# A SwiGLU step's two input products by seven block products of a 2x2 splitting

## The chip, the cores and the metric

One core of one Trainium2 chip, with TensorE (matmul), VectorE (DVE), ScalarE (ACT), GpSimd (POOL) and SyncE (SP, which issues most DMAs). The metric is device time in microseconds, measured in three runs: median 1006.16 us, from 1006.01 to 1006.53.

## The reference, cut to what matters

A decoder layer for 512 tokens of width 1024. It has two macaron half steps; each is a SwiGLU with 2816 hidden features. The second one is

```
h = h + 0.5 * swiglu(rmsnorm(h, g_ffn2), w1_b, w3_b, w2_b)
def swiglu(x, w1, w3, w2):
    return (jax.nn.silu(x @ w1) * (x @ w3)) @ w2
```

Before it stand the first half step and a mixer (attention beside a state-space model); after it a gated embedding and a last norm. Everything is float32. `w1` makes the gate product, `w3` the linear product; together they are 2 x 1024 x 2816 weights.

## The kernel before

Activations lie with features on the 128 partitions and the 512 tokens along the row. A float32 product is made of three TensorE products in a rounded format: each operand is split into a high part (rounded) and a low part (what is left), and `mm3` (lines 234 to 237) adds hi x hi, lo x hi and hi x lo in PSUM. So one block of 128x128 weights costs three matmuls, each with its own weight load. The normalized input is `n3.hl[k]`, k from 0 to 7, with high and low part side by side; the norm's factor per token, `nrm.r`, is multiplied in after the product.

The 2816 hidden features are 22 tiles of 128, in three parts of 7, 7 and 8 (`PARTS`). For each tile there is a unit for the gate product and one for the linear product, each of two steps (4 of the 8 k each, 12 matmuls of 512 columns a step). After a part's tiles come eight products with the second matrix `w2`, which add to the residual tiles `X[m]`. `ffn_units` (line 345) builds the units.

The order of all engines' work is written out by `run` (line 204): for each step it issues first the roundings of the next unit's weights (`split_w`, line 151: a ScalarE cast to the high part), then the evictions that are due (`evicts`), the generators in `chains`, the deferred work in `posts`, then the remainders of the weights (a VectorE subtraction to the low part, which is followed by the next weight DMA on SP), and then the step's matmuls. Each engine takes its instructions in this order and waits for semaphores where data are not there yet. Raw weights go through five buffers of 128x512 (`wraw`), rounded ones through four pairs (`whi`, `wlo`). After a tile's gate product, VectorE multiplies by `nrm.r` (`gate_a`), ScalarE takes tanh, VectorE forms the gate (`gate_b`), and after the linear product follow `lin_a`, `lin_b` and `lin_c`, with a ScalarE cast of the hidden tile between. GpSimd has no work in the second half step, apart from a norm's power.

The gate weights of the gated embedding (`u_g`) are rounded ahead, in units 20 to 15 from the end of the second half step (`U2[j // 2 - 20].extra`). At its end `last` (line 1372 on) makes one tile's product in two halves of 256 columns, with the same three terms.

Of the kernel before, what the change touches and what calls it, by code (L numbers as in the profile page):

```python
# [21 lines left out]
EPS = 1e-6  # L22
FIRST = [(0, 2), (2, 4), (4, 8)]
PREP = 5
FEW = 3
SCORES = [(n, n + 1, n + 2) for n in (0, 4, 8, 12)]
VALUES = [7, 11, 15, 18]
# [14 lines left out]
def hybrid_trunk_kernel(ctx: ExitStack, tc: tile.TileContext, xT, pT, w13a, w2a, w13b, w2b, wqk, wv, ws, wf,  # L42
# [71 lines left out]
    selr = const.tile([128, 8], F32R, name="selr")  # L114


    qsel = [const.tile([128, L], F32R, name=f"qsel{j}") for j in range(2)]
    kcum = [const.tile([128, L], F32R, name=f"kcum{j}") for j in range(2)]
    HALF = [slice(0, 64), slice(64, 128)]


# [1 line left out]
    class Unit:  # L123
        def __init__(self, srcs, steps, posts=(), need=None, alloc=None, ahead=True):
# [3 lines left out]
            self.parts = [None] * len(srcs)  # L128
            self.starts, self.extra = [], []

        def w(self, c, n=1):
            hi, lo = self.parts[c // 4]
            sl = slice((c % 4) * 128, (c % 4 + n) * 128)
            return hi[:, sl], lo[:, sl]

    RAWS = 5
    wseq, raws = [], {}
    dma_at = [0]

    def wdma():  # L140
        j = dma_at[0]
        if j >= len(wseq):
            return
        dma_at[0] += 1
        u, i = wseq[j]
        n = u.srcs[i].shape[-1]
        w = pool.tile([128, 512], F32, name=nm("wraw"), tag="wraw", bufs=RAWS)
        nc.sync.dma_start(w[:, 0:n], u.srcs[i])
        raws[(id(u), i)] = w

    def split_w(u, i):
        w = raws.pop((id(u), i))
        n = u.srcs[i].shape[-1]
        if u.alloc is not None:
            hi, lo = u.alloc()
        else:
            hi = pool.tile([128, 512], F32R, name=nm("whi"), tag="whi", bufs=4)
            lo = pool.tile([128, 512], F32R, name=nm("wlo"), tag="wlo", bufs=4)
        S.copy(hi[:, 0:n], w[:, 0:n])  # L159
        u.parts[i] = (hi, lo)  # L160

        def rest():
            tt(lo[:, 0:n], w[:, 0:n], raw32(hi[:, 0:n]), SUB)
            wdma()
        return rest

    evicts, posts, chains, low, late = [], [], [], [], []
# [19 lines left out]
    def convert(u, nxt, h):  # L187

        last = h == len(u.steps) - 1
        res = []  # L190
        if nxt is not None:
            res = [(nxt, i) for i in range(len(nxt.srcs)) if nxt.parts[i] is None and (i == h or last)]
        return res + [(v, i) for hh, v, i in u.extra if hh == h]

    def order_weights(units):
        seen = set()
        for u, nxt in zip(units, units[1:] + [None]):
            for h in range(len(u.steps)):
                for v, i in convert(u, nxt, h):
                    if (id(v), i) not in seen:  # L200
                        seen.add((id(v), i))
                        wseq.append((v, i))

    def run(units):
        while dma_at[0] < RAWS:
            wdma()
        for ui, u in enumerate(units):
            nxt = units[ui + 1] if ui + 1 < len(units) else None
            for f in u.starts:
                f()  # L210
            for h, step in enumerate(u.steps):
                rest = [split_w(v, i) for v, i in convert(u, nxt, h)] if u.ahead else []
                run_posts(evicts)
                advance(chains)
                while late:
                    late.pop(0)()
                run_posts(posts)
                for f in rest:
                    f()
                step(u)  # L220
                if not u.ahead:
                    for v, i in convert(u, nxt, h):
                        split_w(v, i)()
                if slot_no[0] % 4 != 3:
                    advance(low)
                advance(chains)
                if slot_no[0] % 4 != 3:
                    advance(low)
                slot_no[0] += 1
                for st_, d, f in u.posts:  # L230
                    if st_ == h:
                        evicts.append((slot_no[0] + d, f, u.need))
# [109 lines left out]

    PARTS = [range(0, 7), range(7, 14), range(14, 22)]

    def ffn_units(nrm, w13, w2, final, skip_first=False):
        units = []
        ready = lambda: nrm.r is not None
        for pi, part in enumerate(PARTS):
            hid = {}
            for f in part:  # L350
                box = {}

                def gate_a(box=box):
                    box["t"] = tmp(base="t1")
                    tt(box["t"], box[0], nrm.r, MUL)
                    box["h"] = tmp(base="th")
                    act(box["h"], box["t"], AF.Tanh, scale=0.5)

                def gate_b(box=box):
                    stt(box["t"], box["h"], 1.0, box["t"], ADD, MUL)  # L360

                def lin_a(box=box):
                    box["u"] = tmp(base="t3")
# [24 lines left out]
                for wi in range(2):  # L388
                    srcs = [w13[f, wi][:, c * 512:(c + 1) * 512] for c in range(2)]
                    units.append(Unit(srcs, gemm_steps(box, wi, nrm.pair, KD), [(1, d, fn) for d, fn in after[wi]], ready))  # L390
            f0, n = part[0], len(part)
            pair = lambda k, hid=hid, f0=f0: (hid[f0 + k][:, 0, :], hid[f0 + k][:, 1, :])
            done = pi == len(PARTS) - 1

            def res(box, m, done=done):
                def f():
                    stt(X[m], box[0], 0.5, X[m], MUL, ADD)
                    if done:
                        final(m)
                return f  # L400

            boxes = [{}, {}]

            def side(m, k0, k1, boxes=boxes, pair=pair, n=n):
                def f(u):
                    if k0 == 0:
                        boxes[m][0] = bank()
                    for k in range(k0, k1):
                        mm3(boxes[m][0], *u.w(m * 4 + k - k0), *pair(k), k == 0, k == n - 1)
                return f  # L410
            for k0, k1 in ((0, 4), (4, n)):
# [1013 lines left out]
    u_proj, p_load, p_prep = proj_units(pp)  # L1425
    u_os = out_units(wout[1], n_s, None)
    u_oa = out_units(wout[0], n_a, lambda m: n3.add(m, X[m]))
    U2 = ffn_units(n3, w13b, w2b, lambda m: n4.add(m, X[m]))
    u_g, g_load, g_last = gate_units(n4, pp)

    def chain_at(u, gen):
# [10 lines left out]
    u_qk[3][0].starts.append(p_load)  # L1442
    u_glu[1].starts.append(p_prep)
    chain_at(U2[0], n3.chain(wait=2))
    chain_at(u_g[0], n4.chain(wait=4, halved=True))
    u_g[0].starts.append(g_load)
    for j in range(12):
        U2[j // 2 - 20].extra.append((j % 2, u_g[j // 2], j % 2))


    fw = [[g4([128, KD, 128], dt, "fw") for dt in (F32, F32R, F32R)] for _ in range(2)]
# [156 lines left out]
```

## Time and profile before

| | |
|---|---|
| median of three runs | 1006.16 us |
| profiled execution | 1005.92 us |
| its span, first to last instruction | 1004.1 us |
| TensorE busy | 992.8 us, 99% |
| VectorE busy | 642.2 us, 64% |
| ScalarE busy | 418.8 us, 42% |
| GpSimd busy | 85.5 us, 9% |

The span and the device time differ by 1.8 us that lie around the instructions. Busy time of TensorE is modelled: matmuls are pipelined, so the time from one start to the next tells its pace, and the duration of one (0.39 us) is longer than that. A releaser behind an arrow is what ended the idle time before an instruction.

### The profile page before, as it was taken

The page shows a single profiled execution, that of the slowest core. Times are in us where ns is not written, and L with a number is a line of the kernel's source. Part 1 is how long each engine was busy: PE and PEld are TensorE (multiplying, and loading weights), DVE is VectorE, ACT ScalarE, POOL GpSimd, SP SyncE. Part 2 cuts the span into 40 slices and gives each one's busy share as a digit, 9 for nine tenths or more (in the row PEclk, how much of TensorE's full clock was granted, in tenths as well). Part 3 has the DMA queues.
Part 4 walks back from the last instruction along what each step waited for, and adds up shares of the span by engine and source line. Part 5 has one row for each costly group of instructions (what it writes and reads, how often), then busy time and mean ns, then how long its engine had stood idle before and what let it go on. Part 6 is the DMA issues. An engine that isn't in the chain of part 4 may idle for free.

```text
span 1004.1 us, 13381 instructions
## 1 busy us (share of the span) xinstructions
PE 992.8 (99%) x4800; PEld 826.8 (82%) x4800; DVE 642.2 (64%) x1252; ACT 418.8 (42%) x793; POOL 85.5 (9%) x87
## 2 busy tenths in 40 slices
PE   9999999999999999999999999999999999999996
PEld 7888888888878889887888888888888888888876
DVE  6668788767755555889987865443454436646443
ACT  6333233332244444469995443322333224434232
POOL 0440000001000001004651010000000000000000
PEclk9999999999999999999999999999999999999998
DMA  6433332323245332212212232333323334533101
GB/s 211 149 93 84 110 103 94 87 82 107 95 109 129 94 95 74 64 64 74 80 59 74 86 114 95 103 92 100 101 89 97 93 105 148 168 103 95 43 36 49
DMA packets 56915, 96.57 MB, mean 96 GB/s; under 512 B 10176, under 2 KB 14912, under 8 KB 56848
## 3 DMA queue, kind: packets, MB, share of 16 engines
q1 hardware_dynamic: 56432, 94.62, 30.9%
q0 software_dynamic: 416, 1.08, 0.4%
q8 instruction: 38, 0.62, 0.3%
q14 instruction: 29, 0.24, 0.1%
HBM read 92.41 MB, written 2.10 MB: 94 GB/s over the span
## 4 chain that ended last, share of the span: by engine, by line
PE 93%; DVE 3%; ACT 2%; issue 1%; DMA 1%; POOL 0%; SPq 0%; POOLq 0%; ACTq 0%; DVEq 0%
PE ps L235 29%; PE ps L237 29%; PE ps L236 29%; PE ps L1487 1%; PE ps L1098 1%; PE ps L1144 1%; PE ps L1143 0%; PE ps L315 0%; PE ps L329 0%; DVE lg L1074 0%; DVE qkhl L74 0%; PE ps L754 0%; DVE wlo L74 0%; PE ps L647 0%; DMA fw<-w13a 0%
## 5 line engine op out<-in xcount | busy, mean ns | idle before, releaser
L235 PE MATMUL ps<-xhl,whi 128*128 128x512 f32 x816 | 320.6, 393 | 0.0
L237 PE MATMUL ps<-xhl,whi 128*128 128x512 f32 x816 | 318.1, 390 | 0.0
L236 PE MATMUL ps<-xhl,wlo 128*128 128x512 f32 x816 | 317.9, 390 | 0.0
L159 ACT CAST whi<-wraw 128x512 fp32r<-128x512 f32 x324 | 195.8, 607 | 240.9 <-PE ps L237 177.7
L74 DVE TENSOR_TENSOR wlo<-wraw,whi 128x512 fp32r<-128x512 f32 x324 | 216.6, 673 | 5.8 <-ACT whi L159 5.6
L237 PEld LDWEIGHTS ps<-xhl,whi 128*128 128x128 f32 x816 | 153.2, 188 | 32.2
L235 PEld LDWEIGHTS ps<-xhl,whi 128*128 128x128 f32 x816 | 153.3, 188 | 32.0 <-issue 1.0
L236 PEld LDWEIGHTS ps<-xhl,wlo 128*128 128x128 f32 x816 | 153.4, 188 | 30.9
L235 PE MATMUL ps<-h,whi 128*128 128x512 f32 x352 | 137.4, 390 | 0.0
L237 PE MATMUL ps<-h,whi 128*128 128x512 f32 x352 | 137.1, 389 | 0.0
L236 PE MATMUL ps<-h,wlo 128*128 128x512 f32 x352 | 137.1, 389 | 0.0
L77 DVE SCALAR_TENSOR_TENSOR x<-ps,x 128x512 f32<-128x512 f32 x48 | 33.2, 691 | 95.2 <-PE ps L237 95.1
L77 DVE SCALAR_TENSOR_TENSOR t<-ps,rbc 128x512 f32<-128x512 f32 x44 | 30.3, 690 | 76.4 <-PE ps L237 76.4
L237 PEld LDWEIGHTS ps<-h,whi 128*128 128x128 f32 x352 | 66.1, 188 | 13.8
L235 PEld LDWEIGHTS ps<-h,whi 128*128 128x128 f32 x352 | 66.1, 188 | 13.7
L236 PEld LDWEIGHTS ps<-h,wlo 128*128 128x128 f32 x352 | 66.1, 188 | 13.6
L74 DVE TENSOR_TENSOR t<-ps,rbc 128x512 f32<-128x512 f32 x44 | 30.4, 690 | 71.2 <-PE ps L237 65.0
L80 ACT ACTIVATE th<-t 128x512 f32<-128x512 f32 x44 | 27.8, 633 | 91.1 <-DVE t L74 91.1
L369 ACT CAST h<-t 128x512 fp32r<-128x512 f32 x44 | 27.4, 622 | 80.6 <-DVE t L74 80.6
L319 POOL TENSOR_TENSOR rc<-ms,mhalf 128x4 f32<-128x4 f32 x6 | 8.1, 1345 | 519.3 <-DVE ms L318 519.3
L1090 POOL TENSOR_SCALAR lg<-lg,rs 128x128 f32<-128x128 f32 (+3 forms) x32 | 37.8, 1196 | 97.8 <-issue 78.6
L80 ACT ACTIVATE xhl<-x,colt 128x512 fp32r<-128x512 f32 x32 | 22.9, 725 | 48.2 <-DVE x L77 41.1
(254 smaller groups left out, 1105.0 us busy)
## 6 DMA issues: line engine op xcount, KB each, us to landing
wraw<-w13b SPq DMA_DIRECT2D x88, 256.0 KB, 2.9
wraw<-w13a SPq DMA_DIRECT2D x84, 256.0 KB, 2.8
wraw<-w2a SPq DMA_DIRECT2D x32, 256.0 KB, 2.7
wraw<-w2b SPq DMA_DIRECT2D x32, 256.0 KB, 2.7
wraw<-wqk SPq DMA_DIRECT2D x16, 256.0 KB, 2.8
wraw<-wout SPq DMA_DIRECT2D x16, 256.0 KB, 2.8
wraw<-wgate SPq DMA_DIRECT2D x16, 256.0 KB, 2.8
wraw<-w2a SPq DMA_DIRECT2D x16, 192.0 KB, 2.4
```

The source lines that it names most:

```text
L74: V.tensor_tensor(out, a, b, op)
L77: V.scalar_tensor_tensor(out, a, s, b, op0, op1)
L80: S.activation(out, in_, f, **kw)
L159: S.copy(hi[:, 0:n], w[:, 0:n])
L235: T.matmul(ps, lh, rh, start=start, stop=False)
L236: T.matmul(ps, ll, rh, start=False, stop=False)
L237: T.matmul(ps, lh, rl, start=False, stop=stop)
L369: S.copy(hl[:, 0, :], box["t"])
L1090: G.tensor_scalar(x, x, rs[h2][:, j:j + 1], None, MUL)
L1098: T.transpose(ps[:, j * 128:(j + 1) * 128], lg[h2][:, j * 128:(j + 1) * 128], ident)
L1144: T.matmul(po[:, j * 128:], vv, pl, start=False, stop=j == 3)
L1487: T.matmul(box0[wi], fw[wi][2 if i == 1 else 1][:, k], n1.pair(k)[i == 2], start=k + i == 0, stop=k + i == KD + 1)
```

## The change

`PLAIN = (4, 0, 0)`: in the second half step the first four tiles of the first part stay as they were; the other 3 + 7 + 8 = 18 tiles are made by `quick_units`. There the two products of a tile are taken as one product of 2x2 blocks: block rows are the gate and the (negated) linear features, the inner dimension is halved (k 0 to 3 and 4 to 7), block columns are the lower and the upper 256 tokens. With A11, A12 the gate weights for the two halves of k, A21, A22 the linear ones, xl, xu and yl, yu the input blocks, the seven products are

| i | weights | times |
|---|---|---|
| 0 | A11 | xl |
| 1 | S1 = A21 + A22 | xl - xu |
| 2 | S2 = S1 + A11 | xu - xl - yu |
| 3 | A12 | yl |
| 4 | S3 = A11 + A21 | yu - xu |
| 5 | S4 = A12 + S2 | yu |
| 6 | A22 | yu - xu + xl - yl |

Each takes 4 k of three matmuls with 256 columns. Products 0, 2, 4 and 6 accumulate in the left half of one PSUM bank, and ScalarE copies the half out after 0 (`p1`), 2 (`u2`) and 4 (`u3`); products 3 and 1, 5 lie in the halves of another bank, the right one copied after 1 (`p5`). VectorE puts the outputs together (`gate_a`, `lin_a`, `gate_c`, `lin_b`), now with one more multiplication by `nrm.r`.

The input sums are made once by `halves`, a chain in the first four tiles. S1, S3 and S4 are made by DMAs that GpSimd issues with `accum_op=ADD`, which read the second summand from HBM; S2 by an addition on GpSimd. When a weight is rounded is set by `SPLIT`, in steps from the tile's first product, and the first adding DMA by `FIRST_ADD`. Raw A11 blocks get two buffers of their own (`spare`); these four buffers hold `qsel` and `kcum` earlier on. Rounded weights use the `m2` buffers besides `whi` and `wlo`, so the gate weights of `u_g` are now rounded in units 8 to 3 from the end.

```diff
+PLAIN = (4, 0, 0)
@@
     def wdma():
+        while dma_at[0] < len(wseq):
+            u, i = wseq[dma_at[0]]
+            ring = "k" if isinstance(u, Quick) and i == 1 else "w"
+            done = rings[ring]
+            if len(done) >= SIZE[ring] and not done[len(done) - SIZE[ring]]:
+                return
...
@@
             for h, step in enumerate(u.steps):
...
+                rest += [f for f in [f() for f in u.hooks.get(h, [])] if f]
                 run_posts(posts)
@@
+    def halves(nrm, goff):
...
+        for k in range(4):
+            xa, xb, ta, tb = [tmp(base="xt") for _ in range(4)]
+            act(xa, X[k], AF.Copy, scale=colt[:, goff + k:goff + k + 1])
+            act(xb, X[k + 4], AF.Copy, scale=colt[:, goff + k + 4:goff + k + 5])
+            G.tensor_tensor(ta[:, 0:HT], xa[:, 0:HT], xa[:, HT:], SUB)
+            G.tensor_tensor(tb[:, 0:HT], xb[:, HT:], xa[:, HT:], SUB)
+            G.tensor_tensor(ta[:, HT:], xb[:, HT:], ta[:, 0:HT], ADD)
+            G.tensor_tensor(tb[:, HT:], ta[:, HT:], xb[:, 0:HT], SUB)
...
+            S.copy(a[:, 0, 0:HT], ta[:, 0:HT])
+            act(a[:, 0, HT:], ta[:, HT:], AF.Copy, scale=-1.0)
+            S.copy(b[:, 0, :], tb)
...
+    def quick_units(nrm, w13, fs, hid, before):
...
+        SPLIT = [-5, -4, -3, -2, 1, 2, 0]
+        FIRST_ADD = -10
...
+        def first_add(n):
+            q = tens[n]
+            return lambda: nc.gpsimd.dma_start(q.raw(A21), q.srcs[A22], accum_op=ADD) and None
...
+                S.copy(hi, src)
+                ops[n, i] = hi, lo
+                if i == 0:
+                    G.tensor_tensor(spare(n % 2), q.raw(A21), q.raw(A11), ADD)
+
+                def rest():
+                    tt(lo, src, raw32(hi), SUB)
+                    if i == 0:
+                        nc.gpsimd.dma_start(q.raw(A11), q.srcs[A21], accum_op=ADD)
+                    elif i == 2:
+                        nc.gpsimd.dma_start(spare(n % 2), q.srcs[A12], accum_op=ADD)
...
+                    for k in range(4):
+                        ks = slice(k * 128, k * 128 + 128)
+                        first = k == 0 and i < 2
+                        T.matmul(out, hi[:, ks], moving(i, k, 0), start=first, stop=False, skip_group_check=i > 1)
+                        T.matmul(out, lo[:, ks], moving(i, k, 0), start=False, stop=False, skip_group_check=i > 1)
+                        T.matmul(out, hi[:, ks], moving(i, k, 1), start=False, stop=k == 3, skip_group_check=i > 1)
...
+            def p1(box=box):
+                box["t"] = tmp(base="t1")
+                S.copy(box["t"][:, 0:HT], box[0][:, 0:HT])
...
+            def u2(box=box):
+                S.copy(box["t"][:, HT:], box[0][:, 0:HT])
...
+            def gate_a(box=box):
+                t = box["t"]
+                tt(t, box[1], t, ADD)
+                tt(t, t, nrm.r, MUL)
+
+            def lin_a(box=box):
+                u = box["u"]
+                tt(u[:, HT:], u[:, HT:], u[:, 0:HT], ADD)
+
+            def gate_b(box=box):
+                box["h"] = tmp(base="th")
+                act(box["h"], box["t"], AF.Tanh, scale=0.5)
+
+            def gate_c(box=box):
+                stt(box["t"], box["h"], 1.0, box["t"], ADD, MUL)
+                tt(box["t"], box["t"], nrm.r, MUL)
+
+            def lin_b(box=box):
+                h, t = box["h"], box["t"]
+                stt(h[:, HT:], box["u"][:, HT:], -0.5, t[:, HT:], MUL, MUL)
+                stt(h[:, 0:HT], box[0][:, 0:HT], -0.5, t[:, 0:HT], MUL, MUL)
...
+            d = (0, 0, 0, 1, 1) if last else (0, 1, 2, 3, 4)
+            u = Unit([], [product(i) for i in range(KINDS)],
+                     [(0, 0, p1), (1, 0, p5), (2, 0, u2), (4, 0, u3), (5, 0, gate_a), (5, 0, lin_a)]
+                     + [(6, e, fn) for e, fn in zip(d, (gate_b, gate_c, lin_b, hid_a, hid_b))])
@@
-    U2 = ffn_units(n3, w13b, w2b, lambda m: n4.add(m, X[m]))
+    U2 = ffn_units(n3, w13b, w2b, lambda m: n4.add(m, X[m]), plain=PLAIN)
@@
+    chain_at(U2[0], halves(n3, G_FFN2))
@@
-        U2[j // 2 - 20].extra.append((j % 2, u_g[j // 2], j % 2))
+        U2[j // 2 - 8].extra.append((j % 2, u_g[j // 2], j % 2))
```

## Rows read from the trace of the kernel before

**Rows 1.** The page's first two parts: busy time of each engine; granted clock in 40 slices.
```profile
PE 992.8 (99%) x4800; PEld 826.8 (82%) x4800; DVE 642.2 (64%) x1252; ACT 418.8 (42%) x793; POOL 85.5 (9%) x87
...
PEclk9999999999999999999999999999999999999998
```

**Rows 2.** The chain that ended last: share of the span by engine.
```profile
PE 93%; DVE 3%; ACT 2%; issue 1%; DMA 1%; POOL 0%; SPq 0%; POOLq 0%; ACTq 0%; DVEq 0%
```

**Rows 3.** One plain tile as a stretch: length, each engine's busy time, clock, DMA share, GB/s.
```profile
642.10:652.98 10.88, 10.88 (x49) 9.01 (x48) 5.78 (x9) 3.63 (x6) 0.00 (x0) 1.00 0.31 93
```

**Rows 4.** In order of time, plain tiles: start, duration (us), engine, line, operation, operands.
```profile
641.67 0.39 PE L237 MATMUL ps<-xhl,whi 128*128 128x512 f32 x1
...
642.10 0.69 DVE L77 SCALAR_TENSOR_TENSOR t<-ps,rbc 128x512 f32<-128x512 f32 x1 [2.75 <-PE ps L237]
...
652.98 0.69 DVE L77 SCALAR_TENSOR_TENSOR t<-ps,rbc 128x512 f32<-128x512 f32 x1 [2.76 <-PE ps L237]
```

**Rows 5.** In order of time, the 256-column matmuls and weight loads at the end.
```profile
990.83 0.28 PE L237 MATMUL ps<-gw,xhl 128*128 128x256 f32 x1
...
996.23 0.28 PE L237 MATMUL ps<-gw,xhl 128*128 128x256 f32 x1
...
990.84 0.19 PEld L235 LDWEIGHTS ps<-gw,xhl 128*128 128x128 f32 x1
```

**Rows 6.** In order of time, VectorE's followers, and gate product to tanh and back.
```profile
465.39 0.69 DVE L74 TENSOR_TENSOR wlo<-wraw,whi 128x512 fp32r<-128x512 f32 x1
465.99 0.68 DVE L77 SCALAR_TENSOR_TENSOR qk<-ps,rbc 128x512 f32<-128x512 f32 x1
...
480.60 0.40 DVE L74 TENSOR_TENSOR pb<-ps,pa 128x256 fp32r<-128x256 f32 x1
480.92 0.41 DVE L74 TENSOR_TENSOR pc<-ps,pc 128x256 fp32r<-128x256 f32 x1
...
960.81 0.69 DVE L77 SCALAR_TENSOR_TENSOR gt<-gt,pp 128x512 f32<-128x512 f32 x1 [1.59 <-ACT gt L80]
961.60 0.69 DVE L74 TENSOR_TENSOR o<-gt,ps 128x512 f32<-128x512 f32 x1
...
647.54 0.69 DVE L74 TENSOR_TENSOR t<-ps,rbc 128x512 f32<-128x512 f32 x1 [2.16 <-PE ps L237]
...
648.26 0.63 ACT L80 ACTIVATE th<-t 128x512 f32<-128x512 f32 x1 [2.78 <-DVE t L74]
...
648.93 0.70 DVE L77 SCALAR_TENSOR_TENSOR t<-th,t 128x512 f32<-128x512 f32 x1
```

**Rows 7.** In order of time, ScalarE operations that follow each other.
```profile
497.03 0.60 ACT L159 CAST whi<-wraw 128x512 fp32r<-128x512 f32 x1
497.54 0.36 ACT L1114 CAST pa<-ps 128x256 fp32r<-128x256 f32 x1
497.80 0.37 ACT L1114 CAST pc<-ps 128x256 fp32r<-128x256 f32 x1
```

**Rows 8.** GpSimd's one 512-wide addition (group by line), and VectorE beside GpSimd work.
```profile
L1380 POOL TENSOR_TENSOR o<-o,gfb 128x512 f32<-128x512 f32 x1 | 1.3, 1295 | 5.3 <-ACT gt L80 5.3
...
473.70 0.96 DVE L74 TENSOR_TENSOR wlo<-wraw,whi 128x512 fp32r<-128x512 f32 x1
...
491.35 1.08 DVE L74 TENSOR_TENSOR wlo<-wraw,whi 128x512 fp32r<-128x512 f32 x1
```

**Rows 9.** DMA issues (KB each, us to landing), and GpSimd's issuing of one.
```profile
wraw<-w13b SPq DMA_DIRECT2D x88, 256.0 KB, 2.9
...
wraw<-w2a SPq DMA_DIRECT2D x16, 192.0 KB, 2.4
...
pr<-pT POOLq DMA_DIRECT2D x2, 256.0 KB, 3.3
...
ct<-ssm_bc SPq DMA_DIRECT2D x1, 512.0 KB, 6.9
...
L1233 POOL DMA_DIRECT2D pr<-pT x2 | 1.2, 602 | 0.0
```

More of the change, by code (lines that the diff above doesn't have):

```diff
@@ L114, in hybrid_trunk_kernel, with spare_tile, spare @@
     selr = const.tile([128, 8], F32R, name="selr")
-    qsel = [const.tile([128, L], F32R, name=f"qsel{j}") for j in range(2)]
-    kcum = [const.tile([128, L], F32R, name=f"kcum{j}") for j in range(2)]
+    def spare_tile(dt, base):
+        return pool.tile([128, L], dt, name=nm(base), tag="spare", bufs=4)
+    qsel = [spare_tile(F32R, "qsel") for _ in range(2)]
+    kcum = [spare_tile(F32R, "kcum") for _ in range(2)]
+    spares = []
+    def spare(i):
+        if not spares:
+            spares.extend(spare_tile(F32, "sum") for _ in range(4))
+        return spares[i]
     HALF = [slice(0, 64), slice(64, 128)]
@@ L129, in __init__ @@
             self.starts, self.extra = [], []
+            self.hooks, self.behind = {}, []
         def w(self, c, n=1):
@@ L136, in hybrid_trunk_kernel, with used, __init__, raw @@
     RAWS = 5
-    wseq, raws = [], {}
+    wseq, raws, where = [], {}, {}
     dma_at = [0]
+    rings = {"w": [], "k": []}
+    SIZE = {"w": RAWS, "k": 2}
     def wdma():
[L141 to L149, printed above, removed]
+        while dma_at[0] < len(wseq):
[4 more added lines that the diff above has]
+                return
+            where[(id(u), i)] = ring, len(done)
+            dma_at[0] += 1
+            n = u.srcs[i].shape[-1]
+            if ring == "k":
+                w = spare(2 + len(done) % 2)
+            else:
+                w = pool.tile([128, 512], F32, name=nm("wraw"), tag="wraw", bufs=RAWS)
+            done.append(False)
+            nc.sync.dma_start(w[:, 0:n], u.srcs[i])
+            raws[(id(u), i)] = w
+    def used(u, i):
+        ring, j = where[(id(u), i)]
+        rings[ring][j] = True
+        wdma()
+    class Quick:
+        def __init__(self, srcs):
+            self.srcs = srcs
+        def raw(self, i):
+            return raws[(id(self), i)]
     def split_w(u, i):
@@ L163, in rest @@
             tt(lo[:, 0:n], w[:, 0:n], raw32(hi[:, 0:n]), SUB)
-            wdma()
+            used(u, i)
         return rest
@@ L191, in convert @@
         if nxt is not None:
-            res = [(nxt, i) for i in range(len(nxt.srcs)) if nxt.parts[i] is None and (i == h or last)]
+            res = [(nxt, i) for i in range(len(nxt.srcs)) if nxt.parts[i] is None and (i == h - (len(u.steps) - 2) or last)]
         return res + [(v, i) for hh, v, i in u.extra if hh == h]
@@ L202, in order_weights @@
                         wseq.append((v, i))
+            wseq.extend(u.behind)
     def run(units):
-        while dma_at[0] < RAWS:
-            wdma()
+        wdma()
         for ui, u in enumerate(units):
@@ L343, in hybrid_trunk_kernel, with lows @@
     PARTS = [range(0, 7), range(7, 14), range(14, 22)]
-    def ffn_units(nrm, w13, w2, final, skip_first=False):
+    HT = L // 2
+    def halves(nrm, goff):
+        nrm.ta, nrm.tb = [None] * 4, [None] * 4
+        for _ in range(2):
+            yield
+        for k in range(4):
[6 more added lines that the diff above has]
+            G.tensor_tensor(tb[:, HT:], ta[:, HT:], xb[:, 0:HT], SUB)
+            for _ in range(4):
+                yield
+            a, b = [g4([128, 2, L], F32R, "xth") for _ in range(2)]
+            nrm.ta[k], nrm.tb[k] = a, b
+            S.copy(a[:, 0, 0:HT], ta[:, 0:HT])
+            act(a[:, 0, HT:], ta[:, HT:], AF.Copy, scale=-1.0)
+            S.copy(b[:, 0, :], tb)
+            def lows(a=a, b=b, ta=ta, tb=tb):
+                tt(a[:, 1, 0:HT], ta[:, 0:HT], raw32(a[:, 0, 0:HT]), SUB)
+                stt(a[:, 1, HT:], ta[:, HT:], -1.0, raw32(a[:, 0, HT:]), MUL, SUB)
+                tt(b[:, 1, :], tb, raw32(b[:, 0, :]), SUB)
+            defer(1, lows)
@@ L346, in ffn_units @@
+    def ffn_units(nrm, w13, w2, final, skip_first=False, plain=None):
         units = []
@@ L349, in ffn_units @@
             hid = {}
+            n_plain = len(part) if plain is None else plain[pi]
             for f in part:
+                if f - part[0] >= n_plain:
+                    units += quick_units(nrm, w13, list(part)[n_plain:], hid, units[-3:])
+                    break
                 box = {}
```

69 lines of the change are left out of this document (added).

## The prediction

> **What bounds the kernel now.** I read the page's first two parts, then the chain of waits, then the stretches of the second macaron step, then single instructions in order of time. In the first part TensorE is busy 99% of the span, and its granted clock is 9 tenths or more in all but the last slice, the higher level (2.4 GHz) [rows 1]. The chain of waits puts 93% of the span on TensorE and 3% on VectorE [rows 2]. So whatever shortens TensorE's stream in the second step shortens the kernel, as long as no other engine becomes late. In one plain tile VectorE is busy 5.78 us and ScalarE 3.63 us of 10.88, GpSimd not at all, and the DMA engines are busy 31% [rows 3]. The reader is to see slack beside a full TensorE. From the eviction of one tile's linear product to that of the next are 10.88 us [rows 4]; between them lie 48 matmuls of 512 columns (2 products, 8 k, 3 terms), so 226.7 ns each.
>
> **TensorE's part.** Removed are 48 matmuls of 512 columns in each of 18 tiles; added are 7 x 4 x 3 = 84 of 256. The kernel has 256-column matmuls with a weight load each at its very end: from 990.83 to 996.23 stand 45 spacings, 120.0 ns each, at the same clock level, and a weight load of 0.19 us fits under it because loads follow each other just as closely [rows 5]. So 84 x 0.120 = 10.08 us against 10.88: 0.80 us a tile, 14.4 us over 18. The operands there are swapped (activations stay, weights move), which doesn't change the shape. Lower bound 113.3 ns (half of 226.7; gain 24.5 us), upper bound the point where nothing is won, 10.88/84 = 129.5 ns. I take 120.
>
> The Trainium skill's "TensorE: Matmul & The Clock Gate" (section "Back-to-back issue gap") gives N/2.4 + 2.5 ns, 215.8 and 109.2 ns here. By it the gain would be an estimated 1.19 us a tile, 21 us in all. The rows differ: both widths carry 13.3 ns over N/2.4, and more instructions pay it more often; the sum goes by the rows.
>
> **What comes beside it.** I call a seventh of a tile a step: 12 matmuls, 1.44 us.
> - VectorE: a 512-wide operation holds the queue 0.60 us (465.39 to 465.99), a 256-wide one 0.32 to 0.33, a dependent pair 0.79 [rows 6]. A tile now has 7 weight remainders, two operations each in `gate_a` and `gate_c`, one in `hid_b` and three halves (`lin_a`, `lin_b`): 12 x 0.60 + 3 x 0.33 + two dependences of 0.19 = 8.6 us of 10.08. Before it was 5.78. It fits, with 1.5 us left.
> - ScalarE: 7 roundings, tanh, `hid_a`: 9 x 0.51, and four 256-wide copies out of PSUM at 0.26 [rows 7]: 5.6 us. It fits.
> - GpSimd: one 128x512 addition, 1.295 us alone, and three DMA issues of 0.60 [rows 8, 9]: 3.1 us. It fits.
> - DMA: the four loads take what they took, 0.31 x 10.88 = 3.4 us of every DMA engine [rows 3]. The three adding DMAs fetch three quarters of that again; an adding DMA isn't in the trace, so between 1 and 2 times a plain one (it must also read what it adds to): 2.5 to 5.1 us. Together 5.9 to 8.5 of 10.1 us.
>
> **The order within a tile decides.** All engines run in order, and the kernel's program order ties them in a ring. Product 4 writes the same PSUM half that `u2` copies after product 2. `u2` stands on ScalarE behind `hid_a` of the tile before, which waits for `lin_b`, which stands on VectorE behind the remainder of product 4's weight, `gate_c`, the remainder of product 6's weight; that one waits for a rounding that stands behind tanh, which waits for `gate_a` of the tile before, which waits for its product 5. One round, from product 4 to product 4: products 4 and 5 2.88; TensorE to VectorE 0.20 (641.67 + 0.23 to 642.10 [rows 4]); `gate_a` 0.79; to tanh 0.72; ScalarE's queue 0.51; to VectorE 0.67; remainder 0.60; `gate_c` 0.79 and 0.60; remainder 0.60; `lin_b` 0.33; to `hid_a` 0.45; queue 0.51; `u2` 0.40 [rows 4, 6, 7]. Sum 10.05 us: just under TensorE's 10.08. The ring has no slack, so every delay on VectorE's or ScalarE's part of it goes straight into TensorE's waits at product 4.
>
> GpSimd's addition is such a delay. Beside GpSimd work, VectorE operations with two SBUF inputs take 0.96 and 1.08 us instead of 0.69 [rows 6, 8]: 0.27 to 0.39 more. In the ring VectorE has one hole between `lin_a` (done 4.80 us after product 4's start) and the remainder of product 6's weight (5.77): 0.97 us for an addition of 1.295, 0.33 too short. So both ways of counting say about 0.33, if the addition starts near the hole: period 10.05 + 0.33 = 10.38, 0.30 over TensorE's own. Bounds: 0 (it interferes with nothing) and 1.295 (the whole of it in VectorE's way, period 11.35). The 15 tiles with a block-product tile ahead of them (2 + 6 + 7) pay: 4.5 us, bounds 0 and 19.
>
> The Trainium skill's "SBUF — State Buffer" (section "SBUF: two separate sides") says that GpSimd and a VectorE operation with two SBUF inputs share a port pair as an exclusive lock, the loser blocked for the whole operation. By that rule the upper bound is reached whenever the addition lands on `gate_c`; the rows show 0.39 at most for one 512-wide operation, and some overlapped ones (465.39, 0.69 us) not stretched.
>
> When does the addition start? When the first adding DMA of its tile has landed. That DMA is issued about at product 4's position + 0.5 us. A plain 256 KB DMA from GpSimd's queue lands after 3.3 us; 64 KB more or less is 0.4 to 0.5 us of a plain load (2.9 against 2.4), so 256 KB read once more is at most about 1.9: landing 3.3 to 5.2 us; a 512 KB load at the busy start took 6.9 [rows 9]. I take 4.0, the nearer row: then the addition starts about 4.6, at the hole. The tightest operand is product 5's sum: five steps (7.2 us) less about 1.9 us that its issue and its use sit off the step starts, so 5.3 us is there for it.
>
> SP's queue: five buffers serve three blocks a tile, so the first block's load follows the use of the block five loads earlier, 16 steps ahead of its tile, and `first_add` comes at 10 ahead: 8.6 us for a landing of 2.9. Nothing is late there, and nothing else waits on SP.
>
> The rest: `halves` adds 16 half-wide GpSimd operations, 12 VectorE and 20 ScalarE ones in the first four (plain) tiles, where VectorE uses 5.78 of 10.88 us; nothing, at most 1 us. The gate weights' loads move from the last tiles to the last eight products of the second matrix: 4 loads per 5.44 us (24 matmuls) where a plain tile has 4 per 10.88, so twice its DMA share, an estimated 62%; nothing. The parts' ends: the last hidden tile is ready some 4.6 us after product 6, and is used 6.8 us after it at the earliest; nothing. Tying `qsel` and `kcum` to a shared buffer costs nothing: attention is over by then.
>
> **The sum** against the profiled execution: span 1004.1 and 1.8 around it, 1005.9; the median of the runs shown is 0.2 higher. 1005.9 - 14.4 + 4.5 + 0.5 for the edges (between 0 and 1) = 996.5, on the median's scale 997.
>
> **Rivals.**
> - A, TensorE alone: GpSimd's addition hides, period 10.08; 1006.2 - 14.4 = 992 (990 to 993). For it: TensorE has always been the bound. Against: a ring of 10.05 leaves nothing for any added delay.
> - B, slower: the adding DMA lands late. From about 4.5 us on, the addition slides out of the hole onto the remainder and `gate_c`, and from 5.3 us on product 5's operand is late too, which blocks ScalarE's queue ahead of the copies that TensorE waits for. Period about 11.35: 15 x 1.27 = 19, 1006 - 14.4 + 19 = 1011 (1003 to 1016). It makes the kernel slower from an extra of 14.4/15 = 0.96 us a tile on, which is a landing of about 4.8 us if the exclusion is whole, about 6 if it is as mild as in rows 8. For it: two DMA reads for one, and DMA engines twice as busy as now. Against: plain 256 KB loads in the middle of the kernel land after 2.9 and 3.3 us [rows 9].
> - C, the DMA engines are the bound: if an added packet took over 2.6 times a plain one (10.08 - 3.4 = 6.7 against 2.5), tiles grow without bound from 10.1; at 4 times 13.5 us, 1052. Nothing in the trace speaks for it.
>
> **Chances and range.** A change of 0.2% (2 us) is about what a measurement can tell. Forecast (993 to 1003, its own range): 0.45. A: 0.17. B: 0.30, of which 0.10 within 2 us of before and 0.20 slower. C: 0.05. Others, spread evenly: 0.03. So faster 0.63, same 0.11, slower 0.26. The range from 990 to 1012 leaves out C, the far end of B and a little below A.
>
> **What would show it.** In the profile after: 256-column matmuls 120 ns apart inside a product; a tile of block products of 10.3 to 10.5 us; TensorE idle some 0.3 us before product 4, put down to the copy `t`; VectorE near 85% in the second step; adding DMAs landing after 4 us, under 60 to 85% DMA share. Wrong would be: matmul spacing over 125 ns; waits of TensorE on a rounded weight instead of on the copy; adding DMAs over 5 us; waits in the plain tiles or at the parts' ends.

## The result, and the profile after

The changed kernel takes 1021.85 us (median of 4, from 1018.07 to 1024.8) against 1006.11 us (median of 4) before. The ratio is 1.0152, with a 95% interval from 1.0135 to 1.0169: slower by 1.5%, where 997 us had been forecast. The profiled execution took 1023.37 us, its span 1021.6, 17.5 us more than before; it is the second slowest of the four, 1.5 us over the median.

The page after, as in [rows 1, 2]: busy time of each engine, then two DMA queues (packets, MB, share of 16 engines' span), then the chain's shares.

```profile
PE 986.0 (97%) x5448; PEld 849.6 (83%) x5448; DVE 718.7 (70%) x1372; ACT 475.2 (47%) x939; POOL 175.2 (17%) x175
...
q1 hardware_dynamic: 56432, 94.62, 30.5%
q0 software_dynamic: 8192, 15.24, 9.0%
...
PE 22%; DMA 9%; issue 3%; ACT 2%; DVE 2%; POOL 1%; POOLq 0%; DVEq 0%; SPq 0%; ACTq 0%
```

The chain of waits can be followed back only to 620.17 us this time, so its shares add up to 39% and not to 100, and TensorE's 22% doesn't compare with the 93% of before. In the stretch that it covers, the last plain tile, the block products and what follows them, DMA has 9 points of the 39, where before it had 1 of 100. TensorE is busy 6.8 us less than before, in a span 17.5 us longer, so it waits. Where it waits, the stretches say (length; busy time of PE, PEld, DVE, ACT, POOL; granted clock; DMA share; GB/s). First a tile's length at the start of the second part and one in the middle of it, then three parts' stretches:

```profile
708.83:718.83 10.00, 10.00 (x86) 10.00 (x85) 5.68 (x10) 5.74 (x13) 4.34 (x4) 1.00 0.68 146
...
744.33:756.33 12.00, 10.26 (x86) 10.05 (x85) 9.87 (x16) 6.26 (x14) 4.05 (x4) 1.00 0.70 153
...
630.00:660.00 30.00, 25.04 (x186) 24.12 (x186) 18.76 (x31) 14.15 (x30) 7.99 (x9) 0.94 0.69 144
710.00:790.00 80.00, 71.99 (x567) 70.75 (x567) 60.20 (x96) 40.98 (x85) 24.15 (x23) 0.96 0.63 137
840.00:930.00 90.00, 80.43 (x619) 77.14 (x619) 71.59 (x116) 47.19 (x97) 24.94 (x25) 1.00 0.65 155
```

A tile that finds everything ready takes 10.00 us, as TensorE's part of the prediction had it; in the middle of a part it takes 12.00, more than the 10.88 of a plain tile [rows 3, 4]. In that tile no engine is full: TensorE works 10.26 of the 12 us, VectorE 9.87. The waits of the whole run that tell of it (who waits at which line, for whom; us in all, times, the longest):

```profile
PE ps L497 <- ACT t L511: 21.5, 13, 3.3
...
ACT whi L444 <- DMA sum<-w13b: 16.3, 8, 3.7
```

L511 is `u2`, the copy that clears the PSUM half for product 4. L497 is the first of a product's matmul lines, L444 a weight's rounding. So TensorE waits for ScalarE, and ScalarE for a sum that a DMA makes. Landing times of the weights' DMAs (KB each, median us from issue):

```profile
wraw<-w13b SPq DMA_DIRECT2D x70, 256.0 KB, 3.4
sum<-w13b POOLq DMA_DIRECT2D x36, 256.0 KB, 5.8
...
wraw<-w13b POOLq DMA_DIRECT2D x18, 256.0 KB, 6.9
```

The POOLq rows are the adding DMAs: S3 and S4 in the first, S1 in the second. They land after 5.8 and 6.9 us, where the plain loads beside them need 3.4 and 4.0 had been forecast. By line, the medians are 5.1 us for S3 (4.5 to 6.3), 6.9 for S4 (4.3 to 9.3) and 6.9 for S1 (5.0 to 8.3).

One such tile in order of time (start, duration, engine, line, operation, what ended the idle time before):

```profile
739.62 1.20 POOL L429 DMA_DIRECT2D wraw<-w13b  x1
...
741.00 0.87 POOL L454 DMA_DIRECT2D sum<-w13b  x1 [0.18 <-issue]
...
746.64 1.39 POOL L447 TENSOR_TENSOR sum<-wraw,sum 128x512 f32<-128x512 f32 x1 [4.77 <-DMA wraw<-w13b]
746.79 1.51 DVE L78 SCALAR_TENSOR_TENSOR th<-t,t 128x256 f32<-128x256 f32 x1
...
748.23 0.41 DVE L78 SCALAR_TENSOR_TENSOR th<-ps,t 128x256 f32<-128x256 f32 x1
748.33 0.62 ACT L444 CAST whi<-sum 128x512 fp32r<-128x512 f32 x1 [2.21 <-DMA sum<-w13b]
748.85 0.61 ACT L444 CAST wq<-sum 128x512 fp32r<-128x512 f32 x1
...
749.37 0.61 ACT L541 CAST h<-th 128x512 fp32r<-128x512 f32 x1
...
749.89 0.36 ACT L511 COPY t<-ps 128x256 f32<-128x256 f32 x1
...
750.31 0.38 PE L497 MATMUL ps<-xth,wq 128*128 128x256 f32 x1 [1.74 <-ACT t L511]
```

S4's adding DMA is issued at 741.00 and landed by 748.33, 7.3 us later, where the prediction had counted 5.3 us as available. ScalarE stands idle for it 2.21 us, with `hid_a` (L541) and `u2` (L511) queued behind; product 4 starts when `u2` is done. At the same time GpSimd's addition (L447), which starts when S1 has landed 7.0 us after its issue, runs over VectorE's `lin_b` (L78): 1.51 us for the half that reads two SBUF tiles, where the mean of this line without an addition beside it is 0.42 (below). The other half, 0.41 us at 748.23, starts when the addition is over (746.64 + 1.39 = 748.03) and so says nothing of it.

The waits bring a second loss, of clock. Three stretches: around one wait, right behind it, and behind another one:

```profile
722.60:725.80 3.20, 0.74 (x5) 0.53 (x5) 1.29 (x2) 2.25 (x5) 0.84 (x1) 0.97 0.46 159
725.80:729.00 3.20, 3.20 (x16) 3.20 (x16) 1.90 (x3) 1.29 (x4) 2.58 (x3) 0.50 0.36 56
...
653.90:657.20 3.30, 3.30 (x18) 3.30 (x18) 2.19 (x4) 0.98 (x3) 1.38 (x2) 0.51 0.55 98
```

After the wait of 2.46 us that ended at 725.52 the granted clock is 0.50, the lower level (1.2 GHz), in the 3.2 us of the second row; the same stands behind the waits that ended at 653.0 and at 762.4. In these three stretches 47 matmuls follow each other at 0.213 us instead of 0.120, which is 4.4 us.

The whole balance of the 18 tiles, from the starts of their 1512 matmuls: 211.5 us. At 0.120 us each they would take 181.4. The 15 gaps over 0.3 us make 24.9 of the difference and 66 spacings near 0.21 us, the 47 among them, make 6.4; the other spacings are 0.119 us on average, which takes off 1.3. Eighteen plain tiles took 195.8.

### The profile page after: what moved, and what is told of

Same layout as the page of the kernel before. It is cut to its first block, busy times and chain, and to the rows that moved or that the text cites. A ratio compares the mean times of both kernels' runs of the same rounds, so it can differ in the third digit from the quotient of the medians.

```text
span 1021.6 us, 15114 instructions
## 1 busy us (share of the span) xinstructions
PE 986.0 (97%) x5448; PEld 849.6 (83%) x5448; DVE 718.7 (70%) x1372; ACT 475.2 (47%) x939; POOL 175.2 (17%) x175
## 3 DMA queue, kind: packets, MB, share of 16 engines
q1 hardware_dynamic: 56432, 94.62, 30.5%
q0 software_dynamic: 8192, 15.24, 9.0%
HBM read 106.56 MB, written 2.10 MB: 106 GB/s over the span
## 5 line engine op out<-in xcount | busy, mean ns | idle before, releaser
L196 ACT CAST whi<-wraw 128x512 fp32r<-128x512 f32 x252 | 150.8, 604 | 161.2 <-PE ps L275 116.8
L75 DVE TENSOR_TENSOR wlo<-wraw,whi 128x512 fp32r<-128x512 f32 (+1 forms) x280 | 191.9, 690 | 23.8 <-ACT whi L444 18.0
L273 PE MATMUL ps<-xhl,whi 128*128 128x512 f32 x528 | 208.3, 395 | 0.0
L275 PE MATMUL ps<-xhl,whi 128*128 128x512 f32 x528 | 205.7, 390 | 0.0
L274 PE MATMUL ps<-xhl,wlo 128*128 128x512 f32 x528 | 205.6, 389 | 0.0
L275 PEld LDWEIGHTS ps<-xhl,whi 128*128 128x128 f32 x528 | 99.1, 188 | 21.0
L273 PEld LDWEIGHTS ps<-xhl,whi 128*128 128x128 f32 x528 | 99.1, 188 | 20.8 <-issue 1.0
L274 PEld LDWEIGHTS ps<-xhl,wlo 128*128 128x128 f32 x528 | 99.2, 188 | 19.9
L78 DVE SCALAR_TENSOR_TENSOR x<-ps,x 128x512 f32<-128x512 f32 x48 | 33.2, 691 | 77.7 <-PE ps L275 77.4
L275 PEld LDWEIGHTS ps<-h,whi 128*128 128x128 f32 x352 | 66.1, 188 | 13.8
L497 PE MATMUL ps<-xth,wq 128*128 128x256 f32 x144 | 42.1, 293 | 14.5 <-ACT t L511 13.4
L497 PE MATMUL ps<-xth,whi 128*128 128x256 f32 x144 | 41.7, 290 | 8.1 <-ACT t L511 8.1
L584 ACT CAST h<-t 128x512 fp32r<-128x512 f32 x26 | 16.2, 622 | 55.0 <-DVE t L75 55.0
L499 PE MATMUL ps<-xth,wq 128*128 128x256 f32 x144 | 41.4, 287 | 0.0
L497 PEld LDWEIGHTS ps<-xth,wq 128*128 128x128 f32 x144 | 27.7, 193 | 16.3 <-ACT t L511 15.1
```

The lines of the kernel that those rows point to most:

```text
L75: V.tensor_tensor(out, a, b, op)
L78: V.scalar_tensor_tensor(out, a, s, b, op0, op1)
L273: T.matmul(ps, lh, rh, start=start, stop=False)
L274: T.matmul(ps, ll, rh, start=False, stop=False)
L275: T.matmul(ps, lh, rl, start=False, stop=stop)
L497: T.matmul(out, hi[:, ks], moving(i, k, 0), start=first, stop=False, skip_group_check=i > 1)
```

## The experiments

Theories, after seeing this. *Late DMA*: the adding DMAs land late, and S4's rounding, in ScalarE's queue ahead of `hid_a` and `u2`, holds up TensorE. *Lock*: GpSimd's addition shuts VectorE out, and the ring, which has no slack, gives that on. *Ring*: the ring of in-order engines was counted too short, and would be over 10.08 us without either. The length of the 18 tiles of block products is the common measure. It comes from one profiled execution of each kernel, while the times are medians; executions of one kernel lie up to 6.7 us apart (the changed kernel), so sums of lengths are checked by the medians below.

| kernel | 18 tiles, us | kernel, us | ratio to before, 95% |
|---|---|---|---|
| before (plain tiles) | 195.8 | 1006.11 | |
| after | 211.5 | 1021.85 | 1.0152 (1.0135 to 1.0169) |
| no adding DMAs | 191.1 | 1002.98 | 0.9963 (0.9947 to 0.9979) |
| plain copies in their place | 197.0 | 1008.50 | 1.0016 (1.0006 to 1.0027) |
| one-column addition | 206.0 | 1015.36 | 1.0085 (1.0059 to 1.0111) |
| neither | 184.4 | 995.84 | 0.9894 (0.9875 to 0.9912) |
| S3, S4 rounded a step later | 190.8 | 1002.61 | 0.9962 (0.9949 to 0.9974) |
| and the addition on VectorE | 187.2 | 999.67 | 0.9930 (0.9917 to 0.9944) |
| and S1's DMA a step or more earlier | 188.9 | 999.88 | 0.9928 (0.9914 to 0.9941) |
| later rounding, early S1, addition on GpSimd | 198.9 | 1010.10 | 1.0037 (1.0023 to 1.0051) |
| addition on VectorE, S2 rounded earlier | 209.4 | 1020.79 | 1.0145 (1.0131 to 1.0158) |
| and S1's DMA one step earlier | 190.3 | 1001.79 | 0.9946 (0.9932 to 0.996) |

The four rows from "no adding DMAs" to "neither" are kernels that leave sums of weights out or incomplete; they measure times alone.

**No adding DMAs.**

```diff
-            return lambda: nc.gpsimd.dma_start(q.raw(A21), q.srcs[A22], accum_op=ADD) and None
+            return lambda: None
-                        nc.gpsimd.dma_start(q.raw(A11), q.srcs[A21], accum_op=ADD)
+                        pass
-                        nc.gpsimd.dma_start(spare(n % 2), q.srcs[A12], accum_op=ADD)
+                        pass
```

> Leaves out the three adding DMAs of each tile (products 2, 4 and 5 use incomplete weight sums); GpSimd's addition stays. If the late landing of the adding DMAs is the cause, no operand is late any more: a block-product tile falls from 11.7 us to between 10.1 and 10.5, TensorE's waits on the copy u2 from 25 us to under 6, and the kernel to 992 to 999 us. If GpSimd's addition in VectorE's way is the cause by itself, tiles stay above 11 us and the kernel above 1008.

Measured: 1002.98 us (1002.41 to 1003.64), 18.9 us under the changed kernel, but above what *late DMA* alone had expected. The remaining waits and, in order of time, the addition over a weight's remainder (L75):

```profile
PE ps L497 <- ACT t L511: 6.8, 9, 0.8
```

```profile
750.92 1.66 POOL L447 TENSOR_TENSOR sum<-wraw,sum 128x512 f32<-128x512 f32 x1 [9.35 <-DVE wq L75]
...
751.35 1.77 DVE L75 TENSOR_TENSOR wlo<-sum,whi 128x512 fp32r<-128x512 f32 x1
...
753.05 0.68 DVE L75 TENSOR_TENSOR wq<-wraw,wq 128x512 fp32r<-128x512 f32 x1
```

The operation under the addition takes 1.77 us, the next one, of the same shape, 0.68. In nine tiles product 4 then starts 0.9 us late. Both theories hold a share: the DMAs the larger one.

**Plain copies in place of the adding DMAs.** All three are changed; the cut shows the first.

```diff
-            return lambda: nc.gpsimd.dma_start(q.raw(A21), q.srcs[A22], accum_op=ADD) and None
+            return lambda: nc.gpsimd.dma_start(q.raw(A21), q.srcs[A22]) and None
...
```

> The same three DMAs from GpSimd's queue, but as plain copies of the same blocks over the same buffers (the sums are not made). If adding is what makes them slow (two reads, 179 ns a packet against 88), they land after 3.3 to 4.5 us instead of 5.8 to 6.9 and the kernel falls to 993 to 1005 us. If GpSimd's queue, its waits, or the DMA traffic makes them slow, they land as late as before and the kernel stays at 1015 to 1024.

Measured: 1008.50 us (1008.13 to 1009.16), under the changed kernel by 13.4 us, but above the 993 to 1005 that this branch had expected. Landing, S4's issue (group by line: us in all, mean ns) and waits:

```profile
sum<-w13b POOLq DMA_DIRECT2D x36, 256.0 KB, 4.1
...
wraw<-w13b POOLq DMA_DIRECT2D x18, 256.0 KB, 4.5
```

```profile
L454 POOL DMA_DIRECT2D sum<-w13b x18 | 9.9, 548 | 15.3 <-DVE wq L75 10.4 <-DVE wlo L75 4.8
```

```profile
PE ps L497 <- ACT t L511: 12.7, 12, 1.1
```

In the same places and from the same queue, a copy lands after 4.1 and 4.5 us where an addition lands after 5.8 and 6.9. So the adding itself costs 1.7 and 2.4 us. The issue is dearer as well: 548 ns for a copy, 985 for the same instruction with the addition (the group of the changed kernel, next block).

```profile
L454 POOL DMA_DIRECT2D sum<-w13b x18 | 17.7, 985 | 9.2 <-DVE wq L75 6.3 <-DVE wlo L75 2.4 <-issue 0.4
```

The copies read as much from HBM as the adding DMAs (106.56 MB in both runs). The packets differ in number: without any of these DMAs the queue has 416, with the copies 4736 and with the adding DMAs 8192.

```profile
q0 software_dynamic: 4736, 15.24, 5.0%
```

So the same 54 transfers take 4320 packets as copies and 7776 as adding DMAs. A packet of that queue takes about as long in either run, 170 ns (5.0% of 16 x 1006.4 us, by 4736) and 180 ns, so an adding DMA keeps the DMA engines busy nearly twice as long as a copy.

At 4.1 us, about the landing that had been forecast, ScalarE waits for a sum only once (0.5 us). Yet the tiles take 197.0 us, 12.6 more than with neither DMAs nor addition (below, 184.4). In the tiles 13 VectorE operations are stretched (here and below: over 0.06 us longer than the usual 0.69 us of 512 columns or 0.42 us of 256), by 13.3 us in all, five of them the first of `gate_c`:

```profile
735.34 1.59 POOL L447 TENSOR_TENSOR sum<-wraw,sum 128x512 f32<-128x512 f32 x1 [2.95 <-DMA wraw<-w13b]
735.70 1.78 DVE L78 SCALAR_TENSOR_TENSOR t<-th,t 128x512 f32<-128x512 f32 x1
```

So what is left reads as the lock; no run takes the addition away and leaves the copies.

**A one-column addition on GpSimd.**

```diff
-                    G.tensor_tensor(spare(n % 2), q.raw(A21), q.raw(A11), ADD)
+                    G.memset(spare(n % 2), 0.0)
+                    G.tensor_tensor(spare(n % 2)[:, 0:1], q.raw(A21)[:, 0:1], q.raw(A11)[:, 0:1], ADD)
```

> The adding DMAs stay; GpSimd's 512-wide addition is cut to one column after a memset, so it reads almost nothing from SBUF but still waits for the same DMA (product 2's and 5's weights are wrong by that). If only the late DMAs matter, the kernel stays at 1015 to 1024 us. If the addition's exclusion of VectorE matters as well, VectorE's lin_b (0.66 us mean now, 0.42 alone) goes back to 0.42 and the kernel falls by 5 us or more; if it is the whole cause, to 992 to 999.

Measured: 1015.36 us (1013.12 to 1017.59). One more line above the matmuls makes L511 L512 here.

```profile
PE ps L498 <- ACT t L512: 18.8, 10, 2.5
```

```profile
L78 DVE SCALAR_TENSOR_TENSOR th<-t,t 128x256 f32<-128x256 f32 x18 | 7.5, 419 | 0.1
```

`lin_b`'s operation is back at 419 ns (662 in the changed kernel), and no VectorE operation of the tiles is stretched any more, so the lock is gone; the waits on `u2` stay. *Lock* alone can't be the cause, but with 6.5 us it has its share.

**Neither.** The two edits together leave TensorE, the ring and the loads, and on GpSimd a memset and a one-column addition.

> Leaves out the adding DMAs and all but one column of GpSimd's addition (after a memset of the buffer), so only the order of TensorE, VectorE and ScalarE remains; the roundings stay where the change has them. If the ring of in-order engines is 10.05 us long as the prediction had it, the tiles run at 10.0 to 10.1 us, TensorE waits under 2 us in all, and the kernel is at 990 to 993 us. If the ring by itself is too long, tiles stay near the 11.0 us of the run without adding DMAs, and the kernel above 1000.

Measured: 995.84 us (995.44 to 996.25), above the 990 to 993 expected of a ring of 10.05 us; tiles of about 10.25 us, and many waits so short that they show only at the weight load:

```profile
PEld ps L498 <- ACT t L512: 3.3, 15, 0.2
```

*Ring* holds 3.0 us of the 30 (184.4 against 181.4). On top of it the adding DMAs cost 21.6 us without the addition (206.0 - 184.4) and 20.4 with it (211.5 - 191.1); the addition costs 6.7 without the DMAs (191.1 - 184.4) and 5.5 with them. 184.4 + 21 + 6 gives the 211.5: the two losses add up. The medians of the kernels say the same with other executions: 19.5 and 18.9 us for the adding DMAs (1015.36 - 995.84, 1021.85 - 1002.98), 7.1 and 6.5 for the addition.

**S3 and S4 rounded a step later.** If the place of S4's rounding in ScalarE's queue is what makes a late DMA costly, moving it behind `u2` cures it with the DMAs as late as they are.

```diff
-        SPLIT = [-5, -4, -3, -2, 1, 2, 0]
+        SPLIT = [-5, -4, -3, -2, 2, 3, 0]
```

> Only the roundings of the weights S3 and S4 come one step later (SPLIT 1 to 2 and 2 to 3), so that S4's rounding stands behind u2 on ScalarE and not ahead of it, with 1.44 us more for its DMA. If ScalarE's queue blocked by the late S4 is what makes TensorE wait, waits on u2 fall from 25 us to under 10 and the kernel to 996 to 1008 us. If the DMAs are late by so much that the operands themselves are the bound, TensorE waits for the rounded weights instead and the time stays above 1013.

Measured: 1002.61 us (1002.01 to 1003.82).

```profile
PE ps L497 <- ACT t L511: 3.4, 3, 1.2
```

```profile
sum<-w13b POOLq DMA_DIRECT2D x36, 256.0 KB, 6.3
...
wraw<-w13b POOLq DMA_DIRECT2D x18, 256.0 KB, 6.9
```

The DMAs land even later for S3 and S4, 6.3 us, and the wait on `u2` falls from 21.5 to 3.4 us. The edit also lets ScalarE ask a step later; that the place counts, and not only the time won, is seen where S4 is late all the same. One tile, `u2` and then S4's rounding:

```profile
748.76 0.37 ACT L511 COPY t<-ps 128x256 f32<-128x256 f32 x1
749.56 0.62 ACT L444 CAST whi<-sum 128x512 fp32r<-128x512 f32 x1 [0.43 <-DMA sum<-w13b]
```

`u2` starts before S4 has landed in 10 of the 18 tiles, by up to 2.0 us; in the changed kernel it never starts less than 1.07 us after the landing, with a rounding, and mostly `hid_a` too, in between. So not the DMA's length in itself cost the time, but that `u2` was queued behind it.

**The addition on VectorE**, with the later rounding.

```diff
-                    G.tensor_tensor(spare(n % 2), q.raw(A21), q.raw(A11), ADD)
+                    V.tensor_tensor(spare(n % 2), q.raw(A21), q.raw(A11), ADD)
```

> The roundings of S3 and S4 one step later, and the addition S2 on VectorE instead of GpSimd (0.60 us there). The output is complete. If GpSimd's exclusion of VectorE costs about 0.9 us a tile, this gains some 5 us on the run with late rounding alone: 995 to 1000 us. If VectorE is full (9.2 of 10.1 us) or waits at the addition for the adding DMA, which lands after 6.9 us, TensorE's waits move to rounded weights and it stays at 1001 to 1008.

Measured: 999.67 us (998.75 to 1000.1). VectorE has the work of one more 512-wide operation, and the kernel gets 2.9 us faster by it; of the 14 stretched VectorE operations of the version before it, none is left. This version beats both the kernel before and the changed one, and of those that make all the sums only the next comes level with it.

```profile
PEld ps L497 <- ACT t L511: 2.2, 8, 0.3
...
PE ps L498 <- DVE wlo L75: 1.5, 3, 0.9
```

**S1's adding DMA earlier**, in that version: at 13 steps ahead of its tile instead of 10 (in a part's first tiles as early as the part's plan lets it).

```diff
-            plan.append((n * KINDS + FIRST_ADD, first_add(n)))
+            plan.append((max(n * KINDS - 13, -10 if n == 0 else -4), first_add(n)))
```

> As the one with S2 on VectorE, and the first adding DMA issued three steps (4.3 us) earlier, so that VectorE doesn't wait for it. Complete output. If the landing of the first adding DMA and GpSimd's addition were what was left, tiles come to 10.1 to 10.3 us: 992 to 996 us, under both kernels. If S4's DMA, issued only after its own rounding, is still late, tiles stay at 10.5 and the kernel at 997 to 1001.

Measured: 999.88 us (997.97 to 1001.16), no better: not the 992 to 996 hoped for, but the 997 to 1001 of the other branch, S4 still late.

```profile
sum<-w13b POOLq DMA_DIRECT2D x36, 256.0 KB, 7.1
...
wraw<-w13b POOLq DMA_DIRECT2D x18, 256.0 KB, 5.2
```

S1 now lands after 5.2 us (7.0 without this edit), and S3 and S4 after 7.1 (6.3): what one adding DMA won, the others lost.

**The same with the addition on GpSimd** (later rounding, early S1).

> Late rounding and the early first adding DMA, with the addition back on GpSimd. Complete output. It starts then when GpSimd's queue comes to it and not when the DMA lands. If GpSimd's exclusion is the cost, this stays 4 to 8 us above the one with S2 on VectorE (998 to 1003 us); if the landing is, the two are within 2 us of each other.

Measured: 1010.10 us (1009.35 to 1011.6); expected were 998 to 1003.

```profile
PE ps L498 <- DVE wlo L75: 6.3, 7, 1.1
...
PE ps L498 <- DVE wq L75: 3.1, 4, 1.0
...
ACT whi L444 <- POOL sum L447: 5.6, 5, 1.4
```

TensorE now waits for a weight's low part. Of VectorE's operations 16 are stretched, 13 of them remainders, by 22.7 us in all, against 14 and 12.6 us in the version with later rounding alone. And the addition itself is late. In the other versions with the whole addition on GpSimd behind S1's DMA it starts within 0.14 us of S1's landing, here a median of some 5.7 us after it: the issue of the next tile's S1, now ahead of it in GpSimd's queue, waits for VectorE or for its block's load (up to 7.1 us inside a part), and ScalarE's rounding of S2 then waits for the addition. So this run doesn't price the lock alone; where the addition falls decides, and the early S1 moved it.

**S2 rounded a step earlier**, in the version with the addition on VectorE, to give S2 and S4 more time.

```diff
-        SPLIT = [-5, -4, -3, -2, 2, 3, 0]
+        SPLIT = [-5, -4, -4, -2, 2, 3, 0]
```

> The version with late rounding and S2 on VectorE, and S2 rounded one step earlier (SPLIT -3 to -4), so that S4's adding DMA is issued up to 1.4 us earlier. Complete output. If what is left of TensorE's and ScalarE's waits (tiles of 10.4 us against 10.25 with neither adding DMA nor addition) is S4's landing, it gains 1 to 3 us on that version's 999.7: 996.5 to 999 us. If VectorE's load of 9.2 us a tile is what is left, it stays within 1 us of 999.7.

Measured: 1020.79 us (1020.72 to 1022.05), ratio 1.0145 (1.0131 to 1.0158): 21 us worse than without it, a clear miss. The order of two issues in GpSimd's queue, first in the version without the edit, then with it, and then the waits:

```profile
839.09 1.19 POOL L429 DMA_DIRECT2D wraw<-w13b  x1
...
841.23 0.88 POOL L454 DMA_DIRECT2D sum<-w13b  x1 [0.95 <-DVE wlo L75]
```

```profile
843.46 0.88 POOL L454 DMA_DIRECT2D sum<-w13b  x1 [0.93 <-DVE wq L75]
844.04 1.19 POOL L429 DMA_DIRECT2D wraw<-w13b  x1
```

```profile
DVE sum L447 <- DMA wraw<-w13b: 31.5, 18, 3.0
...
PE ps L498 <- DVE wq L75: 9.7, 7, 2.2
```

S4's DMA (L454) waits for S2's remainder on VectorE. It is now issued ahead of the next tile's S1 (L429), which leaves behind it; S1 is late, and VectorE's addition waits for it in all 18 tiles, 31.5 us, with all of VectorE's queue behind.

**The same with S1 one step earlier**, which restores the order.

```diff
-            plan.append((n * KINDS + FIRST_ADD, first_add(n)))
+            plan.append((max(n * KINDS - 11, -10 if n == 0 else -4), first_add(n)))
```

> As the one before, and the first adding DMA issued one step (1.4 us) earlier. Complete output. If S1's landing then holds VectorE's addition, which comes earlier relative to it, this gains another 1 us (995.5 to 998.5). If the earlier issue only crowds the DMA engines, as three steps earlier seemed to (S3 and S4 landed after 7.1 instead of 6.3 us), it is level with the one before or up to 2 us slower.

Measured: 1001.79 us (999.21 to 1002.26), ratio 0.9946 (0.9932 to 0.996). 19 us come back. S1 is not earlier than it was without both edits: its issue comes 13.8 us ahead of its tile's first product (median), against 13.9 without them and 13.4 with the first alone. So what came back is the order, and the order was the cause. It isn't faster than without both edits. Of the 7.7 us between 999.67 and TensorE's own bound as rival A gave it (992), none of the later orders won any.

## Why the prediction was wrong

It put the late landing of the adding DMAs at nothing and the addition's hold on VectorE at 4.5 us; the runs showed 19 to 22 us for the first, and up to 12.6 for the second.

- **TensorE's part was right.** Of the 1512 matmuls' spacings some 1430 lie between 0.11 and 0.13 us, and a tile with nothing to wait for took 10.00 us (10.08 forecast). The formula that I set beside the rows, N/2.4 + 2.5 ns, is in the Trainium skill's "TensorE: Matmul & The Clock Gate" (section "Back-to-back issue gap") the gap of an isolated matmul, not of a stream with weight loads; the stream here kept to the rows' 120 ns.
- **The ring was right within 0.2 us a tile.** Counted as 10.05 us, under TensorE's 10.08; with both delays removed, tiles took some 10.25, 3.0 us over 18 tiles. That it has no slack, and that delays in it would show as waits of product 4 on `u2`, was right: product 4 waits there at its first matmul in 13 tiles.
- **The landing of the adding DMA is the step that failed:** "A plain 256 KB DMA from GpSimd's queue lands after 3.3 us; 64 KB more or less is 0.4 to 0.5 us of a plain load (2.9 against 2.4), so 256 KB read once more is at most about 1.9: landing 3.3 to 5.2 us [...] I take 4.0, the nearer row". It measured 5.8 and 6.9 us, above the upper end. Two parts were off. A copy in that place took 4.1 to 4.5 us, not 3.3: that row is from another stage of the kernel. And the adding added 1.7 to 2.4 us, where I had taken 0.7. The "5.3 us" for S4 was near (in the tile shown ScalarE came to it 5.1 us after its issue) and with 4.0 left 1.3 to spare; with 6.9 the margin is negative, and the term I set at 0 became 20 to 22 us of the tiles (19 by the medians).
- **GpSimd's addition is a second term that failed, sized by the wrong rows:** 0.30 us a tile and 4.5 us in all were forecast. Beside the late DMAs it cost 5.5 us and without any DMAs 6.7, which looks near but is luck. With copies that land after 4.1 and 4.5 us, about as forecast, the tiles took 12.6 us more than with neither, the addition fell on `gate_c` and the remainders instead of the hole, and the kernel took 1008.50 us: a right landing alone would not have brought the 997. The 0.39 of [rows 6, 8] isn't the limit of one collision: operations under the addition took 1.51 us instead of 0.41 to 0.42, and 1.77 instead of 0.68. The Trainium skill's "SBUF — State Buffer" (section "SBUF: two separate sides"), whose rule of an exclusive lock I had set against the rows, is what this trace shows: 1.1 us lost by each of these two operations, beside additions of 1.39 and 1.66 us.
- **Rival B named the mechanism**, in its place and with its point of decision (a landing of 4.8 to 6 us), and was given 0.30. It said 11.35 us a tile and 1011; measured were 11.75 (211.5 / 18) and 1022, above its own 1016. What it lacked is the second loss, 4.4 us at the lower clock behind long waits, and that waits reached 3.3 us where the whole addition was to be its price.
- **Rival A** would have been closest with both obstacles away (995.84 against 992); **rival C** didn't occur: the DMA share stayed at 0.61 to 0.70 in the tiles.
- **The rest was right.** The three parts' eight products with `w2` take 38.1, 38.1 and 43.5 us before and after. From the last of them to the end are 58.7 us against 57.6. The four plain tiles end at 631.6 us against 631.0, and 0.5 of these 0.6 us are there at 69 us already, long before the second half step. So 30.0 lost in the tiles, less 14.4 won, plus 1.1 and 0.6, gives 17.3 of the 17.5 us.

What stays open: how the longer landing of an adding DMA parts among the 1.8 times as many packets, the longer issue and the addition itself; no run separates these.

## What to carry to other kernels

When a change adds an operation that the trace doesn't show, and an in-order queue with no slack stands behind it, forecast from the far bound of its time (here even that, 5.2 us, was short of the 5.8 to 6.9 measured), and ask first what is queued behind the instruction that will wait for it: here a one-step move of that instruction won back 19 us with the DMA as slow as it was. An instruction that waits for another engine, put ahead of DMA issues in the same queue, delays these by its wait; moving one issue past another cost 21 us. And an addition that looks free on an idle GpSimd can be dearer than the same one on a busy VectorE, since both shut each other out when both read SBUF.

## What the runs showed of the hardware

- An adding DMA of 256 KB, issued by GpSimd, lands after 5.8 to 6.9 us, a copy in its place after 4.1 to 4.5. Its issue mostly holds GpSimd for 0.87 to 1.20 us instead of 0.55. It takes 144 packets where a copy takes 80 (7776 and 4320 for 54). A packet on that queue took 180 ns (9.0% of 16 x 1021.6 us, by 8192), 170 with copies, on the other queue 88 ns (30.5%, by 56432).
- An addition on GpSimd and a VectorE operation that reads two SBUF tiles exclude each other; one that reads PSUM isn't stretched (with later rounding, 0.42 us at 747.73, within an addition that runs from 747.45 for 1.52 us).
- Behind gaps of 2.07, 2.74 and 3.54 us from one matmul's start to the next, TensorE's granted clock was 0.50 or 0.51 in stretches of 3.2 to 3.4 us, though it had been 0.97 or more before; in the stretch from 840 to 930, with gaps of up to 2.35 us, it stayed at 1.00.
